# Hybrid attention and recurrence trunk: a block's value products run together, a head's first two sums run together

## The chip, the cores and the metric

One core of one Trainium2 chip runs the whole program. The metric is the device time of one execution in microseconds (us); for a kernel it is the median of its runs. A profile of one further execution gives the times of single instructions.

The engines are named as in the profile: PE is TensorE (matmuls), DVE VectorE, ACT ScalarE, POOL GpSimd, SP SyncE, which here issues DMAs alone.

## The reference, cut to what matters

Two layers over 1024 tokens of width 1024, float32. Each layer normalizes its input, projects it to 5376 columns, runs two mixers beside each other, gates and merges them, and projects back.

```python
p = jnp.exp(s - m)                                       # s: scores in windows of 128 tokens, masked
p = p / (jnp.sum(p, axis=-1, keepdims=True) + jnp.exp(sink - m))
o = jnp.einsum('bhgnqk,bnkhd->bnqhgd', p, vb)            # attention's value products, 8 heads of 64
...
decay = jnp.exp(jnp.where(causal, diff, MASK_VALUE))     # recurrence, 4 heads of 128
scores = jnp.einsum('bhtd,bhsd,bhtsd->bhts', qc, kc, decay)
o = (jnp.einsum('bhts,bhsv->bhtv', scores, vc)
     + jnp.einsum('bhtd,bhdv->bhtv', qc * jnp.exp(G), S))
...
merged = (jax.nn.sigmoid(gate_attn) * (a @ w_up_attn[layer])
          + jax.nn.sigmoid(gate_hgrn) * (b @ w_up_hgrn[layer]))
x = x + merged @ w_out[layer]
```

## The kernel before, in words

Every float32 projection is split into a high and a low part and computed as three matmuls of 128x512 into one accumulator. These are the "full" matmuls of the texts below: 128 rows and 128 columns of weights, 512 columns of data. They carry names that begin with `pi`, `pj` or `pu` in the stages of this change.

A layer goes through these stages: norm and transposes, the paired projections (`pair`), attention (`attend`, called from a loop over eight blocks of 128 tokens, together with the projection `value(u)` that makes `pi`), the four heads of the recurrence (`core`), the merge, and the output projection. In the loop over blocks, step u computes the transposes of block u-4 (`turn`), the value products of block u-4 (`values`), the scores of block u-1 and the softmax of block u-2. From block 4 on, the projections of the recurrence's first head (`pj_f`, `pj_qh`) stand beside attention in place of `pi`.

In `turn`, the probabilities of a block are transposed on PE in two groups of four heads (`tp`), group 0 and group 1, one per key-value head. ACT copies a group's transposes to `pT[:, 0]`, and DVE multiplies them with a mask into `pT[:, 1]`; in block 0 the masked one alone is used. In `values`, each group is multiplied with `vn` and `vd` (the values, and the difference of neighbouring blocks' values) into one PSUM bank `av`. An output has 64 rows, so the weights have 64 columns, and the two halves r = 0 and 1 fill the two halves of the bank.

In `core`, a head's intra-chunk scores are built level by level on DVE (`gs`, `pairs`, then `grow`), with sums over the partitions on PE. The first two of these sums (`near`, shown as `lv_n`) have a matrix of ones with 32 columns as weights: first `gs` and then `pairs` (a part of the tile `tab`), each in four quarters q. The later levels are `lv` (32 columns), `lv_m` (32), and `l` (32 and then 64). The heads are interleaved: head h starts five steps after head h-1, and the generator `filling()` gives the full matmuls of the other projections between the steps.

What sets the order: the code is written with a tile framework that keeps dependences between tiles and has a scheduler, which moves instructions of each engine ahead of one another when the operands that an instruction needs are due later. So the order on an engine isn't that of the code. At run time each engine runs its own list strictly in that order, and waits on semaphores. PSUM tiles come from two pools: `pj` (3 banks, projections) and `ps` (5 banks, all others, `av`, `sc`, `tp`, `lv_n` among them).

Of the kernel before, what the change touches and what calls it, by code (L numbers as in the profile page):

```python
# [14 lines left out]
ALU = mybir.AluOpType  # L15
AX = mybir.AxisListType

P = 128
# [6 lines left out]
HD = 64  # L25
# [15 lines left out]
def trunk_kernel(ctx, tc, x, positions, norm_w, w_in, attn_sinks, hgrn_norm_w, w_up_attn,  # L41
# [3 lines left out]
    V, S, G, PE = nc.vector, nc.scalar, nc.gpsimd, nc.tensor  # L45
# [11 lines left out]
    def slot(shape, name, dt=F32):  # L57
        return sp.tile(shape, dt, tag="slot", name=name)

    def bank(shape, name):  # L60
        return ps.tile(shape, F32, tag="bank", name=name)


    def bcast_row(row, nm):
# [6 lines left out]
    idle = slot([P, P], "idle")  # L71
    V.memset(idle, 0.0)
    zeros = bank([P, 4, P], "zeros")
    for j in range(18):
        PE.matmul(zeros[:, j % 4], lhsT=idle, rhs=idle, start=True, stop=True)
# [106 lines left out]
    def norm_turn_soon(ys, hT, hF, b0, nm, wt=None):  # L182
# [3 lines left out]
        for g in range(2):  # L186
            for b, y in enumerate(ys, b0):
                tp = bank([P, 4, P], f"tp_{nm}_{b}_{g}")
                for j in range(4):
                    k = 4 * g + j  # L190
                    PE.transpose(tp[:, j], y[:, k * P:(k + 1) * P], ident)
                tps.append((b, g, tp))
# [24 lines left out]
    def norm_turn(ys, hT, hF, b0, nm):  # L217

        n = 0
        for b, y in enumerate(ys, b0):  # L220
            a, o = b // 4, (b % 4) * P
            n += 1
            for g in range(2):
                tp = bank([P, 4, P], f"tp_{nm}_{b}_{g}")
                for j in range(4):
                    k = 4 * g + j
                    PE.transpose(tp[:, j], y[:, k * P:(k + 1) * P], ident)
                for j in range(2):
                    S.copy(hF.t[a][2 * g + j][:, :, o:o + P], tp[:, 2 * j:2 * j + 2])
        a, o = b0 // 4, (b0 % 4) * P  # L230
        t = slice(o, o + n * P)
        for kp in range(KT // 2):
            S.copy(hT.hi[a][kp][:, :, t], hF.t[a][kp][:, :, t])
            V.tensor_tensor(out=hT.lo[a][kp][:, :, t], in0=hF.t[a][kp][:, :, t],
                            in1=hT.hi[a][kp][:, :, t].bitcast(F32), op=ALU.subtract)
# [267 lines left out]
    pairs = [tuple((qkv[j][0], j) for j in js) for js in ((0, 1), (3, 2), (4, 5))]  # L503
# [11 lines left out]
    for L in range(DEPTH):  # L515
# [90 lines left out]
        other = []  # L606
# [60 lines left out]
        for g in range(2):  # L667
# [4 lines left out]
        ones, side, upper, never, mdiag, mlev, sink, hnw, lb, oml = (  # L672
            made[n] for n in "ones side upper never mdiag mlev sink hnw lb oml".split())
# [41 lines left out]
        probs = {}  # L715
# [43 lines left out]
        def turn(b):  # L759
            pr, _ = probs[b]  # L760
            probs[b] = []
            for g in range(2):

                tp = bank([P, 2, 2, P], f"tp_{L}_{b}_{g}")
                for j in range(4):
                    PE.transpose(tp[:, j % 2, j // 2], pr[:, 4 * g + j], ident)
                pT = slot([P, 2, 4, P], f"pT_{L}_{b}_{g}")
                whole = tp.rearrange("p r i q -> p (r i) q")
                if b:
                    S.copy(pT[:, 0], whole)  # L770
                V.tensor_tensor(out=pT[:, 1], in0=whole, in1=side.unsqueeze(1).broadcast_to([P, 4, P]), op=ALU.mult)
                probs[b].append(pT)

        def values(b):
            av = bank([P, 4, P], f"av_{L}_{b}")
            for g, pT in enumerate(probs.pop(b)):
                for pt in ([0, 1] if b else [1]):
                    for r in range(2):
                        PE.matmul(av[r * HD:(r + 1) * HD, 2 * g:2 * g + 2].rearrange("p h q -> p (h q)"),  # L779
                                  lhsT=(vd if b and pt else vn[0])[:, b - 1 if b else 0, g * HD:(g + 1) * HD],  # L780
                                  rhs=pT[:, pt, 2 * r:2 * r + 2].rearrange("p h q -> p (h q)"),
                                  start=pt == 0 or b == 0, stop=pt == 1)
            d = hp.tile([P, 4, P], F32, tag="po", name=f"avo_{L}_{b}")
            S.copy(d, av)
            nc.scalar.dma_start(ad[:, :, b * P:(b + 1) * P], d)

        def before(u):
            if u > 3:
                turn(u - 4)

        def attend(u):
            if u > 3:
                values(u - 4)
            if 0 < u <= NB:
                scores(u - 1)
            if 1 < u <= NB + 1:
                softmax(u - 2)
# [85 lines left out]
        def core(h):  # L883
# [3 lines left out]
            f1, R, Q = (slot([P, T], f"{n}_{nm}") for n in ("f1", "R", "Q"))  # L887
# [36 lines left out]
            def grow(hh):  # L924
# [5 lines left out]
            near = bank([P, NB, 48], f"lv_{nm}_n")  # L930
            V.tensor_tensor(out=gs, in0=R, in1=Q, op=ALU.mult)
            V.tensor_tensor(out=Q, in0=Q, in1=f1, op=ALU.mult)
            pairs = tab[:, 512:1024]
            V.tensor_tensor(out=pairs, in0=R.rearrange("p (n j) -> p n j", j=2)[:, :, 0],
                            in1=Q.rearrange("p (n j) -> p n j", j=2)[:, :, 1], op=ALU.mult)
            for src, n, o in ((gs, 32, 0), (pairs, 16, 32)):
                for q in range(4):
                    PE.matmul(near[q * 32:(q + 1) * 32, :, o:o + n], lhsT=ones,
                              rhs=src.rearrange("p (c q n) -> p q c n", q=4, n=n)[:, q], start=True, stop=True)
            yield  # L940
            V.tensor_tensor(out=acc, in0=near[:, :, 0:32], in1=mdiag.unsqueeze(1).broadcast_to([P, NB, 32]),
                            op=ALU.mult)
# [7 lines left out]
                            in0=R.rearrange("p (n i) -> p n i", i=4)[:, :, 0:2].unsqueeze(3)  # L950
                            .broadcast_to([P, T // 4, 2, 2]),
                            in1=Q.rearrange("p (n j) -> p n j", j=4)[:, :, 2:4].unsqueeze(2)
                            .broadcast_to([P, T // 4, 2, 2]), op=ALU.mult)
            lvs = bank([P, 2, NB, 32], f"lv_{nm}_1")
            for q in range(4):
                PE.matmul(lvs[q * 32:(q + 1) * 32, 0], lhsT=ones, rhs=kn[:, :, q * 32:(q + 1) * 32],
                          start=True, stop=True)
# [20 lines left out]
            for u in range(2):  # L978
                S.copy(X[u][:, :, 16:32], Qh[u][:, :, 1])
                V.tensor_tensor(out=X[u][:, :, 32:48], in0=Qh[u][:, :, 1],  # L980
                                in1=F.rearrange("p (u n j) -> p u n j", u=2, j=4)[:, u, :, 1:2]
# [3 lines left out]
            for c in range(NB):  # L985
                for q in range(4):
                    o = c * P + q * 32
                    PE.matmul(lvm[q * 32:(q + 1) * 32, c], lhsT=R[:, o:o + 32], rhs=X[c // 4][:, c % 4 * 4 + q],
                              start=True, stop=True)
# [13 lines left out]
            for c in range(NB):  # L1003
                for q in (0, 2):
                    o = c * P + q * 32
                    PE.matmul(l32[q * 32:(q + 1) * 32, c], lhsT=R[:, o:o + 32], rhs=Q[:, o + 32:o + 64],
                              start=True, stop=True)
# [5 lines left out]
            for c in range(NB):  # L1013
                o = c * P
# [15 lines left out]
            for g in range(2):  # L1030
                kv = bank([P, 4, P], f"kv_{nm}_{g}")
                n = 4 if g == 0 else 3
                for j in range(n):
                    c = 4 * g + j
                    PE.matmul(kv[:, j], lhsT=kn[:, c], rhs=it[:, c], start=True, stop=True)
                for j in range(n):
                    c = 4 * g + j
                    if c == 0:
                        V.tensor_copy(SS[:, 1], kv[:, 0])
                    else:  # L1040
                        V.scalar_tensor_tensor(out=SS[:, c + 1], in0=SS[:, c], scalar=F[:, c:c + 1],
                                               in1=kv[:, j], op0=ALU.mult, op1=ALU.add)
# [5 lines left out]
            for g in range(2):  # L1048
                po = bank([P, 4, P], f"po_{nm}_{g}")
                for j in range(4):  # L1050
                    c = 4 * g + j
# [51 lines left out]
        fill = filling()  # L1103

        heads, done = [core(h) for h in range(NHG)], 0
        for t in range(25):
            for h in range(NHG):
# [203 lines left out]
```

## Time and profile before

| | |
|---|---|
| median of 3 runs | 1406.21 us (1405.28 to 1406.41) |
| the profiled execution's own time | 1405.02 us |
| its span, first to last instruction | 1403.2 us |
| mean granted TensorE clock | 0.997 of full speed |
| busy: PE, DVE, ACT, POOL | 1379.4, 999.9, 694.6, 111.1 us |
| matmul records on PE | 8108 |
| attention, first scores to last value products, layers 1 and 2 | 328.5 to 423 us, 1017 to 1113 us |
| recurrence, first product of head 0 to last transposes of head 3 (`tb`), layers 1 and 2 | 430 to 582 us, 1120 to 1272 us |

A row of the profile's timeline has the start (us from the span's beginning), the length, the engine, the line, the operation with the tile written and the tiles read, the shape, and how many records were merged into the row; idle time of the engine before it stands in brackets. For a matmul, 128*64 is rows and columns of weights. [...] The end of a matmul is modelled and overlaps the next one's start, so the distance between starts is what a matmul takes on the queue.

### The profile page before, as it was taken

The page shows a single profiled execution, that of the slowest core. Times are in us where ns is not written, and L with a number is a line of the kernel's source. Part 1 is how long each engine was busy: PE and PEld are TensorE (multiplying, and loading weights), DVE is VectorE, ACT ScalarE, POOL GpSimd, SP SyncE. Part 2 cuts the span into 40 slices and gives each one's busy share as a digit, 9 for nine tenths or more (in the row PEclk, how much of TensorE's full clock was granted, in tenths as well). Part 3 has the DMA queues.
Part 4 walks back from the last instruction along what each step waited for, and adds up shares of the span by engine and source line. Part 5 has one row for each costly group of instructions (what it writes and reads, how often), then busy time and mean ns, then how long its engine had stood idle before and what let it go on. Part 6 is the DMA issues. An engine that isn't in the chain of part 4 may idle for free.

```text
span 1403.2 us, 21296 instructions
## 1 busy us (share of the span) xinstructions
PE 1379.4 (98%) x8108; PEld 1122.0 (80%) x8108; DVE 999.9 (71%) x1638; ACT 694.6 (49%) x1386; POOL 111.1 (8%) x195
## 2 busy tenths in 40 slices
PE   8999999999999999999999999999999999999997
PEld 7878888888777878888878888888887778788885
DVE  6867668843746879599976666776356378877998
ACT  8754334444785654313665333344358656352254
POOL 1100013220000001000010001122100000100000
PEclk9999999999999999999999999999999999999998
DMA  9434477875236651771264345587913466329203
GB/s 289 164 128 143 135 222 209 258 278 185 79 110 197 224 187 63 279 255 36 83 209 151 99 148 176 173 257 220 332 68 99 135 211 218 114 83 398 105 0 121
DMA packets 204278, 240.04 MB, mean 171 GB/s; under 512 B 14288, under 2 KB 140752, under 8 KB 204176
## 3 DMA queue, kind: packets, MB, share of 16 engines
q1 hardware_dynamic: 156528, 145.08, 31.5%
q10 hardware_dynamic: 34944, 52.44, 10.4%
q0 software_dynamic: 12704, 41.17, 9.2%
q8 instruction: 64, 1.05, 0.3%
q14 instruction: 38, 0.31, 0.1%
HBM read 160.00 MB, written 78.64 MB: 170 GB/s over the span
## 4 chain that ended last, share of the span: by engine, by line
PE 89%; ACT 4%; DVE 4%; DMA 1%; issue 1%; ACTq 0%; DVEq 0%; SPq 0%
PE pb L303 6%; PE pb L304 6%; PE pb L305 6%; PE pc L303 4%; PE pc L304 4%; PE pc L305 4%; PE pg L265 2%; PE pg L267 2%; PE pg L266 2%; PE pj_qh L141 2%; PE av L779 2%; PE pj_qh L143 2%; PE pj_qh L142 2%; PE pi L806 2%; PE pi L805 2%; PE pi L807 2%
## 5 line engine op out<-in xcount | busy, mean ns | idle before, releaser
L130 ACT CAST whi_s<-ws 128x1024 fp32r<-128x1024 f32 x30 | 31.6, 1054 | 89.4 <-PE pc L305 89.0
L314 DVE TENSOR_TENSOR pq<-pc,pq 128x512 f32<-128x512 f32 x37 | 25.5, 690 | 61.4 <-PE pc L305 56.3
L130 ACT CAST whi_o<-wo 128x1024 fp32r<-128x1024 f32 x20 | 21.1, 1055 | 78.7 <-PE pu_uh L143 35.5
L539 ACT ACTIVATE pq<-pq 128x512 f32<-128x512 f32 x60 | 37.9, 631 | 44.1 <-DVE pq L314 42.6
L141 PE MATMUL pu_ua<-wh_a,wlo_ua 128*128 128x512 f32 x128 | 52.4, 409 | 0.0
L130 ACT CAST whi_t<-ws 128x1024 fp32r<-128x1024 f32 x30 | 31.6, 1055 | 41.8 <-PE pc L305 27.9
L265 PE MATMUL pg<-hh,wl_p 128*128 128x512 f32 (+1 forms) x128 | 47.4, 373 | 4.9 <-ACT p L269 3.6
L143 PE MATMUL pu_ua<-wh_a,whi_ua 128*128 128x512 f32 x128 | 50.6, 395 | 0.0
L142 PE MATMUL pu_ua<-wl_a,whi_ua 128*128 128x512 f32 x128 | 50.4, 394 | 0.0
L131 DVE TENSOR_TENSOR wlo_s<-ws,whi_s 128x1024 fp32r<-128x1024 f32 x30 | 36.7, 1223 | 18.7 <-ACT whi_s L130 18.7
L141 PE MATMUL pu_uh<-wh_b,wlo_uh 128*128 128x512 f32 x128 | 49.8, 389 | 0.0
L143 PE MATMUL pu_uh<-wh_b,whi_uh 128*128 128x512 f32 x128 | 49.8, 389 | 0.0
L142 PE MATMUL pu_uh<-wl_b,whi_uh 128*128 128x512 f32 x128 | 49.8, 389 | 0.0
L754 ACT ACTIVATE pr<-pr,mx 128x128 f32<-128x128 f32 x128 | 49.7, 392 | 0.1
L303 PE MATMUL pb<-th,wl 128*128 128x512 f32 x120 | 47.2, 393 | 0.5 <-ACT pq L344 0.4
L303 PE MATMUL pb<-th,wlo_s 128*128 128x512 f32 x120 | 47.1, 392 | 0.0
L1001 POOL COPY scT<-acc 32x256 f32<-32x256 f32 x32 | 23.5, 734 | 296.7 <-DVE acc L995 180.6
L303 PE MATMUL pc<-hh,wlo_t 128*128 128x512 f32 x120 | 46.9, 390 | 0.0
L304 PE MATMUL pb<-tl,wh 128*128 128x512 f32 x120 | 46.8, 390 | 0.0
L305 PE MATMUL pc<-hh,whi_t 128*128 128x512 f32 x120 | 46.8, 390 | 0.0
L305 PE MATMUL pb<-th,wh 128*128 128x512 f32 x120 | 46.7, 390 | 0.0
L305 PE MATMUL pb<-th,whi_s 128*128 128x512 f32 x120 | 46.7, 390 | 0.0
(423 smaller groups left out, 4463.4 us busy)
## 6 DMA issues: line engine op xcount, KB each, us to landing
wr<-in_w_in_dram SPq DMA_DIRECT2D x72, 512.0 KB, 4.6
gd<-pq ACTq DMA_DIRECT2D x79, 256.0 KB, 3.3
fq<-fq ACTq DMA_DIRECT2D x48, 256.0 KB, 2.1
wr_p<-in_w_in_dram SPq DMA_DIRECT2D x23, 512.0 KB, 6.0
x<-in_x_dram SPq DMA_DIRECT2D x16, 512.0 KB, 6.1
qs<-qsd POOLq DMA_DIRECT2D x16, 512.0 KB, 8.2
u<-gd SPq DMA_DIRECT2D x16, 512.0 KB, 10.1
ga<-gd SPq DMA_DIRECT2D x16, 512.0 KB, 10.2
```

The costliest lines, as they stand in the source:

```text
L130: S.copy(hi, raw)
L131: eng.tensor_tensor(out=lo, in0=raw, in1=hi.bitcast(F32), op=ALU.subtract)
L141: PE.matmul(acc, lhsT=ll, rhs=rh, start=i == 0, stop=False)
L142: PE.matmul(acc, lhsT=lh, rhs=rl, start=False, stop=False)
L143: PE.matmul(acc, lhsT=lh, rhs=rh, start=False, stop=i == n - 1)
L265: PE.matmul(acc, lhsT=wl[:, k], rhs=h[:, t], start=k == 0, stop=False, skip_group_check=q > 0)
L266: PE.matmul(acc, lhsT=wh[:, k], rhs=l[:, t], start=False, stop=False, skip_group_check=q > 0)
L303: PE.matmul(acc, lhsT=wl[:, k], rhs=h, start=start and k == 0, stop=False, skip_group_check=not start)
L304: PE.matmul(acc, lhsT=wh[:, k], rhs=l, start=False, stop=False, skip_group_check=not start)
L305: PE.matmul(acc, lhsT=wh[:, k], rhs=h, start=False, stop=k == 3, skip_group_check=not start)
L539: S.activation(d, src, AF.Sigmoid if r < 2 * KT else AF.Silu)
L754: S.activation(pr[:, h], pr[:, h], AF.Exp, bias=mx[:, h:h + 1], accum_out=sm[:, h:h + 1])
```

## The change

A helper `wait_too` lets one instruction wait for a second one's result beside its own operands. It is used at two places. In `values`, blocks 0 to 5, every matmul of group 0 also waits for the masked product of group 1 (`own`), the last operand of the block. In `core`, every matmul of the first sum also waits for the product `pairs`, the operand of the second. No arithmetic and no operand changes.

```diff
+    def wait_too(ins, other):
+
+        tc.add_manual_dep(ins.ins, other.ins.name,
+                          mybir.DependencyInfo(mybir.DependencyClass.Sync, mybir.DependencyReason.DATA),
+                          reason="together")
...
-                V.tensor_tensor(out=pT[:, 1], in0=whole, in1=side.unsqueeze(1).broadcast_to([P, 4, P]), op=ALU.mult)
+                own = V.tensor_tensor(out=pT[:, 1], in0=whole, in1=side.unsqueeze(1).broadcast_to([P, 4, P]),
+                                      op=ALU.mult)
                 probs[b].append(pT)
+            probs[b].append(own)
...
-            for g, pT in enumerate(probs.pop(b)):
+            *pTs, own = probs.pop(b)
+            for g, pT in enumerate(pTs):
...
-                        PE.matmul(av[r * HD:(r + 1) * HD, 2 * g:2 * g + 2].rearrange("p h q -> p (h q)"),
+                        mm = PE.matmul(av[r * HD:(r + 1) * HD, 2 * g:2 * g + 2].rearrange("p h q -> p (h q)"),
...
+                        if g == 0 and b < 6:
+                            wait_too(mm, own)
...
-            V.tensor_tensor(out=pairs, in0=R.rearrange("p (n j) -> p n j", j=2)[:, :, 0],
+            paired = V.tensor_tensor(out=pairs, in0=R.rearrange("p (n j) -> p n j", j=2)[:, :, 0],
                             in1=Q.rearrange("p (n j) -> p n j", j=2)[:, :, 1], op=ALU.mult)
...
+                    mm = PE.matmul(near[q * 32:(q + 1) * 32, :, o:o + n], lhsT=ones,
+                                   rhs=src.rearrange("p (c q n) -> p q c n", q=4, n=n)[:, q], start=True, stop=True)
+                    if o == 0 and h > -1:
+                        wait_too(mm, paired)
```

The scheduler then makes another order. In both layers it is the same change. On PE in the attention stage, block 3 of layer 1: `av_3` are the value products of block 3 (group 0 reads `pT_3_0`, group 1 `pT_3_1`), `sc_6` the scores of block 6, `pi_7` and `pj_f` full matmuls. Before:

```order
L807 MATMUL pi_7_3476<-wh_i_6_2866,hh_1_3_179 128x512
L779 MATMUL av_3_3504<-pT_3_0_3465,vn_2689 64x256 x2
L779 MATMUL av_3_3504<-pT_3_0_3465,vd_2844 64x256 x2
L779 MATMUL av_3_3504<-pT_3_1_3473,vn_2689 64x256 x2
L730 MATMUL sc_6_0_0_3518<-ks_0_0_2870,qs_0_0_2874 128x256
L730 MATMUL sc_6_0_1_3519<-ks_0_1_2872,qs_0_1_2876 128x256
L779 MATMUL av_3_3504<-pT_3_1_3473,vd_2844 64x256 x2
L734 MATMUL sc_6_0_0_3518<-ks_0_1_2872,qs_0_0_2874 128x256
```

The same place on PE now:

```order
L149 MATMUL pj_f_0_0_0_3587<-hh_0_3_175,wh_f_0_3351 128x512
L147 MATMUL pj_f_0_1_0_3697<-hhi_0_2882,wl_f_0_3352 128x512
L788 MATMUL av_3_3504<-pT_3_0_3465,vn_2689 64x256 x2
L788 MATMUL av_3_3504<-pT_3_0_3465,vd_2844 64x256 x2
L788 MATMUL av_3_3504<-pT_3_1_3473,vn_2689 64x256 x2
L788 MATMUL av_3_3504<-pT_3_1_3473,vd_2844 64x256 x2
L736 MATMUL sc_6_0_0_3518<-ks_0_0_2870,qs_0_0_2874 128x256
L736 MATMUL sc_6_0_1_3519<-ks_0_1_2872,qs_0_1_2876 128x256
```

The four pairs of value products stand in one piece, the scores behind them, and the piece stands 25 full matmuls later.

On PE in the recurrence stage, head 3 of layer 1: `lv_3_n` are its first two sums (from `gs_3` and from `tab_3`), `l_0_2` matmuls of 64 columns of head 2, `pu_ua` full matmuls. Before, the sum from `gs_3` stood eleven full matmuls ahead of this piece:

```order
L142 MATMUL pu_ua_1_1_5011<-wl_a_1_1_4564,whi_ua_0_4805 128x512
L143 MATMUL pu_ua_1_1_5011<-wh_a_1_1_4563,whi_ua_0_4805 128x512
L1015 MATMUL l_0_2_5028<-Q_2_4630,R_2_4629 64x64
L938 MATMUL lv_3_n<-tab_3_4983,ones 32x8x16 x4
L1015 MATMUL l_0_2_5028<-Q_2_4630,R_2_4629 64x64 x7
L141 MATMUL pu_ua_2_0_5059<-wh_a_0_0_4276,wlo_ua_2_5054 128x512
```

The same place on PE now:

```order
L149 MATMUL pu_ua_1_1_5011<-wh_a_1_1_4563,whi_ua_0_4805 128x512
L147 MATMUL pu_ua_2_0_5059<-wh_a_0_0_4276,wlo_ua_2_5054 128x512
L148 MATMUL pu_ua_2_0_5059<-wl_a_0_0_4277,whi_ua_2_5053 128x512
L149 MATMUL pu_ua_2_0_5059<-wh_a_0_0_4276,whi_ua_2_5053 128x512
L949 MATMUL lv_3_n<-gs_3_4982,ones 32x8x32 x4
L949 MATMUL lv_3_n<-tab_3_4983,ones 32x8x16 x4
L1028 MATMUL l_0_2_5028<-Q_2_4630,R_2_4629 64x64 x8
```

Both sums and head 2's `l` stand in one piece, three full matmuls later than the second sum stood and fourteen later than the first.

More of the change, by code (lines that the diff above doesn't have):

```diff
@@ L937, in core @@
                 for q in range(4):
-                    PE.matmul(near[q * 32:(q + 1) * 32, :, o:o + n], lhsT=ones,
-                              rhs=src.rearrange("p (c q n) -> p q c n", q=4, n=n)[:, q], start=True, stop=True)
+                    mm = PE.matmul(near[q * 32:(q + 1) * 32, :, o:o + n], lhsT=ones,
+                                   rhs=src.rearrange("p (c q n) -> p q c n", q=4, n=n)[:, q], start=True, stop=True)
+                    if o == 0 and h > -1:
+                        wait_too(mm, paired)
             yield
```

## The prediction

> **What bounds the kernel now.** I read the page's busy times and its chain first, then the waits of TensorE, then TensorE's timeline at the two places that the change touches. Of the page:
>
> ```profile
> span 1403.2 us, 21296 instructions
> PE 1379.4 (98%) x8108; PEld 1122.0 (80%) x8108; DVE 999.9 (71%) x1638; ACT 694.6 (49%) x1386; POOL 111.1 (8%) x195
> PE 89%; ACT 4%; DVE 4%; DMA 1%; issue 1%; ACTq 0%; DVEq 0%; SPq 0%
> ```
>
> TensorE is busy for 98% of the span and makes 89% of the chain that ended last. So time taken out of TensorE's own queue comes off the end, as long as nothing it waits for becomes late. The list of its waits is short; the rows that belong to the stages of this change are
>
> ```profile
> PE tb L1068 <- DVE tab L1059: 1.3, 2, 0.7
> PE lv_n L938 <- DVE gs L931: 0.5, 1, 0.5
> ```
>
> (us in total, times, longest). In two layers of attention and recurrence TensorE stands still there for about 2 us. A busy share hides a second kind of loss, though, which is what this change is about: the price of a short run of column-tiled matmuls between full ones. TensorE's timeline around the value products (`av`, 128*64 weights) of one block shows it. Columns: start, length, line, what it does, records merged into the row. Each f32 matmul leaves two records.
>
> ```profile
> 361.14 0.39 PE L806 MATMUL pi<-wlo_i,hhi 128*128 128x512 f32 x1
> 361.46 0.65 PE L779 MATMUL av<-pT,vn 128*64 128x256 f32 x4
> 362.04 0.51 PE L730 MATMUL sc<-ks,qs 128*128 128x256 f32 x2
> 362.38 0.40 PE L734 MATMUL sc<-ks,qs 128*128 128x256 f32 x2
> 362.62 0.40 PE L730 MATMUL sc<-ks,qs 128*128 128x256 f32 x2
> ...
> 363.10 0.40 PE L807 MATMUL pi<-whi_i,hhi 128*128 128x512 f32 x1
> 363.33 0.40 PE L805 MATMUL pi<-wh_i,hl 128*128 128x512 f32 x1
> 363.66 0.65 PE L779 MATMUL av<-pT,vd 128*64 128x256 f32 x4
> 364.14 0.60 PE L779 MATMUL av<-pT,vn 128*64 128x256 f32 x4
> 364.58 0.60 PE L779 MATMUL av<-pT,vd 128*64 128x256 f32 x4
> 365.11 0.50 PE L730 MATMUL sc<-ks,qs 128*128 128x256 f32 x2
> 365.45 0.40 PE L734 MATMUL sc<-ks,qs 128*128 128x256 f32 x2
> ```
>
> Read starts, not lengths, since matmuls overlap. Undisturbed, a full matmul takes 0.23 us (363.10 to 363.33), a pair of `sc` records 0.24 (362.38 to 362.62), and four `av` records inside a run 0.44 (364.14 to 364.58). The lone run of four takes, from the full matmul ahead to the second `sc` row behind, 361.14 to 362.38 = 1.24 us. Take off 0.23 + 0.44 + 0.24 and 0.33 us is left. The run of twelve: 363.33 to 365.45 = 2.12, less 0.23 + 3 × 0.44 + 0.24, leaves 0.33. So a run of column-tiled matmuls costs a fixed third of a microsecond whatever its length. It lies on TensorE's queue in the open: about 0.09 on entry (0.32 from 361.14 to the run where 0.23 is usual), the rest inside and on the way out, where the first pair of `sc` records takes 0.34 (365.11 to 365.45) instead of 0.24.
>
> The recurrence pays the same. Head 0's two sums over the partitions (`lv_n`, 128*32 weights):
>
> ```profile
> 431.76 0.39 PE L142 MATMUL pj_f<-hl,whi 128*128 128x512 f32 x1
> 432.08 0.64 PE L938 MATMUL lv_n<-gs,ones 128*32 128x256 f32 x8
> 432.65 0.50 PE L143 MATMUL pj_f<-hh,whi 128*128 128x512 f32 x1
> 432.99 0.39 PE L141 MATMUL pj_f<-hh,wlo 128*128 128x512 f32 x1
> ...
> 434.38 0.39 PE L141 MATMUL pj_qh<-hh,wlo 128*128 128x512 f32 x1
> 434.69 0.43 PE L938 MATMUL lv_n<-tab,ones 128*32 128x128 f32 x8
> ...
> 435.39 0.39 PE L143 MATMUL pj_qh<-hh,whi 128*128 128x512 f32 x1
> ```
>
> 431.76 to 432.99 less two full matmuls is 0.77 us for the first sum, 434.38 to 435.39 less two is 0.55 for the second. By the steady rate, 0.44 and 0.22, the fixed part is again 0.33 in each.
>
> **The change part by part.** No arithmetic is added or removed; each engine issues the same instructions, and SP's and POOL's queues keep their order. What changes is the order on TensorE, and behind it on DVE and ACT.
>
> *Value products.* In program order each of blocks 0 to 5 now has one run. Runs before, by block 0 to 7: 2, 2, 4, 2, 1, 2, and 4 for blocks 6 and 7 together; that is 17 a layer. Now: six times 1, and 5 for blocks 6 and 7, which have no added wait but are cut differently; 11 a layer. Six runs × 0.33 = 2.0 us a layer.
>
> *First two sums of a head.* Heads 0 and 1: two runs become one, 0.33 each. In heads 2 and 3 the `l` matmuls (128*64 weights) of the head before join:
>
> ```profile
> 498.92 0.64 PE L938 MATMUL lv_n<-gs,ones 128*32 128x256 f32 x8
> 499.48 0.49 PE L143 MATMUL pj_qh<-hh,whi 128*128 128x512 f32 x1
> 499.91 1.15 PE L1015 MATMUL l<-Q,R 128*64 128x64 f32 x16
> 501.32 0.39 PE L142 MATMUL pj_qh<-hlo,whi 128*128 128x512 f32 x1
> 503.03 0.43 PE L938 MATMUL lv_n<-tab,ones 128*32 128x128 f32 x8
> ...
> 528.93 0.39 PE L143 MATMUL pu_ua<-wh_a,whi_ua 128*128 128x512 f32 x1
> 529.25 0.33 PE L1015 MATMUL l<-Q,R 128*64 128x64 f32 x2
> 529.65 0.43 PE L938 MATMUL lv_n<-tab,ones 128*32 128x128 f32 x8
> 531.30 0.40 PE L142 MATMUL pu_ua<-wl_a,whi_ua 128*128 128x512 f32 x1
> ```
>
> Head 2: the `l` run takes 499.48 to 501.32 less two full matmuls, 1.38, of which 0.1 is a wait (0.43 to its start where 0.32 is usual); so 1.28, and 0.95 without the fixed part. Head 3, where `l` was cut by the second sum: 528.93 to 531.30 less two is 1.91; less 0.95, 0.22 and 0.33, two changes between 64 and 32 columns cost 0.41, 0.2 each. The new run (sum, sum, `l`) has one such change: 0.44 + 0.22 + 0.95 + 0.33 + 0.2 = 2.14. It replaces 0.77 + 1.28 + 0.55 = 2.60 in head 2 and 0.77 + 1.91 = 2.68 in head 3: 0.46 and 0.54. The four heads give 0.33 + 0.33 + 0.46 + 0.54 = 1.7 us a layer.
>
> The Trainium skill (TensorEngine Tiling, section Key Properties) says that changing the tiling mode, not just the tile, drains the engine. By that rule the change from 32 to 64 columns within the new run is paid for, as the 0.2 from head 3's rows also has it; if only steps to and from the full array were paid for, the four such changes would be free and the saving 0.8 us larger. The row decides, and agrees with the rule.
>
> Both stages, both layers: 2 × (2.0 + 1.7) = 7.4 us off TensorE's queue. In all 88 runs become 66.
>
> *What the added waits cost.* A run's first matmul now needs the last operand of the whole run, and all of TensorE's queue stands behind it. What covers this is full matmuls moved ahead of the run. Rows for the last operands (DVE):
>
> ```profile
> 361.87 1.28 DVE L771 TENSOR_TENSOR pT<-tp,side 128x512 f32<-128x512 f32 x2
> 430.36 1.23 DVE L931 TENSOR_TENSOR gs<-R,Q 128x1024 f32<-128x1024 f32 x1 [6.05 <-DMA Q<-fq]
> 433.36 0.69 DVE L934 TENSOR_TENSOR tab<-R,Q 128x512 f32<-128x512 f32 x1
> 501.64 0.68 DVE L934 TENSOR_TENSOR tab<-R,Q 128x512 f32<-128x512 f32 x1
> 528.91 0.68 DVE L934 TENSOR_TENSOR tab<-R,Q 128x512 f32<-128x512 f32 x1
> ```
>
> Block 1: its run stands 11 full matmuls later than its first part did: 361.46 + 11 × 0.23 - 0.33 (block 0's saving) = 363.66; the second product ends at 361.87 + 1.28 = 363.15. Covered by 0.5. Block 0 has five full matmuls between its second transposes and its run, where it had two, and blocks 2 to 5 have 15 to 36 (3.4 us or more). Head 0: the new run stands at 434.69 - 0.77 + 14 × 0.23 = 437.1, the pair product ends at 434.05: covered. Head 2: 503.03 - 0.77 - 1.38 + 6 × 0.23 = 502.26, the product ends at 502.32: a wait of some 0.1 with its signal. Head 3: 529.25 - 0.77 + 3 × 0.23 = 529.17, the product ends at 529.59: a wait of 0.4, with the signal 0.5 (before, the second sum started 0.06 after the product's end). Head 1 lies between head 0 and head 2; I take nothing. Two layers: 2 × 0.6 = 1.2 us given back. Bounds: 0 if DVE comes earlier by as much, 3 us if every one of the 20 runs with an added wait waits 0.15.
>
> *Waits that go.* In layer 2, head 1's first sum waited for its operand:
>
> ```profile
> 1145.52 0.64 PE L938 MATMUL lv_n<-gs,ones 128*32 128x256 f32 x8 [0.53 <-DVE gs L931]
> ```
>
> It now stands 16 full matmuls (3.7 us) later, so the 0.5 goes, and so does head 2's 0.1 in each layer: 0.7, or nothing if the pair product there comes as late. Behind the runs, the next sums and transposes keep their place to within a dozen full matmuls, and from each head's `lv_m` on the order is as before but for one matmul in head 0, so the 1.3 us at `tb` stays: it depends on the distance from TensorE's own `po`, not on the clock on the wall.
>
> Sum: -7.4 + 1.2 - 0.7 = -6.9 us. The profiled execution took 1405.02 us (span 1403.2 and 1.8 around it) and would take 1398.1. The median of the three runs before is 1406.21, 1.2 above it; against that I predict 1399.3 us. The runs before spread over 1.1 us, so I take 0.2% (2.8 us) as what a measurement can tell from no change.
>
> **The rivals.**
>
> *The added waits eat half.* For: the cover at block 1 and in heads 1 to 3 is half a microsecond or less, and DVE's and ACT's orders change too. Against: nearly every run has full matmuls moved ahead of it. With 0.15 us of waiting in each of the 20 runs that got a wait, the 3 us above, and nothing gone: 1406.2 - 7.4 + 3 = 1401.8.
>
> *All cover holds, and more goes.* No new waits, the 0.7 gone and half a microsecond of small gaps with it: 1406.2 - 7.4 - 1.2 = 1397.6.
>
> *The fixed part does not go with the run.* If the 0.33 belonged to the matmuls (their first pass, say) and not to the change of tiling, joining runs would save nothing: 1406.2. Against: four and twelve records leave the same rest, and the pieces inside the twelve follow each other at 0.44.
>
> *Slower: the pair product decides.* Place: the merged sums of all eight heads. DVE's products for the two sums lie 430.36 to 434.05, 3.7 us, apart in head 0, and DVE has its other work between them. If the second is a further 2 us late in each head (three DVE operations of 0.68 put ahead of it), TensorE waits 8 × 2 = 16 us and the kernel ends at 1406.2 - 6.9 + 16 = 1415. It decides from 6.9/8 = 0.9 us a head on. Against: head 0 has 3 us to spare, and in the worst place, head 3, I find 0.5. The Trainium skill (TensorE: Matmul & The Clock Gate, Part 3) has matmuls start and end strictly in program order, so nothing behind would slip past such a wait; the row at 1145.52 agrees, since TensorE stood idle for 0.53 us there with full matmuls next in its queue.
>
> **How the numbers follow.** Forecast (1398 to 1400.6): 0.60. Half eaten (1400.6 to 1403): 0.20. More goes (below 1398): 0.10. No saving: 0.05. Slower: 0.05. The limit for faster is 1403.4, which the first and third cases keep and nine tenths of the second: 0.60 + 0.10 + 0.18 = 0.88. Within 0.2%: 0.05 + 0.02 = 0.07. Slower: 0.05. The range leaves out the last two and the far ends of the others: 1397.2 to 1402.2, its upper end the bound of 3 us plus the runs' own spread of half a microsecond.
>
> **What would show it.** Right: 66 column-tiled runs, each with a rest of about 0.33 us over the steady rates; TensorE's busy time down by some 7 us; new short waits at `lv_n` in heads 2 and 3 (under 1 us each), none at `av`. Wrong in the waits: `lv_n` or `av` high in TensorE's list of waits. Wrong in the price: the same gain missing with no waits there, the runs' rests above 0.4 us. Wrong further on: `lv`, `tn` or `tb` waiting for DVE for more than the 1.3 us of before.

## The result, and the profile after

The changed kernel took 1398.99 us (median of four runs, 1398.09 to 1400.56), the kernel before 1406.12 beside it (1405.28 to 1406.41): a ratio of 0.995, 95% interval 0.9939 to 0.9962. A second comparison gave 1397.82 against 1405.30: 0.9947 (0.9935 to 0.996). Predicted were 1399.3 us.

The page of the changed kernel, then its TensorE waits (us in total, times, longest):

```profile
span 1398.8 us, 21263 instructions
PE 1372.1 (98%) x8108; PEld 1123.6 (80%) x8108; DVE 996.6 (71%) x1638; ACT 695.6 (50%) x1386; POOL 111.0 (8%) x195
PE 85%; DVE 5%; ACT 4%; DMA 3%; issue 1%; SPq 1%; DVEq 0%; ACTq 0%
```

```profile
PE lv_n L949 <- DVE tab L945: 2.8, 5, 1.1
PE tb L1081 <- DVE tab L1072: 1.3, 2, 0.7
```

TensorE's busy time is down by 7.3 us (1379.4 to 1372.1) with the same 8108 records, and the wait at `lv_n` is up from 0.5 us to 2.8, now for `tab`, the pair product. `av` isn't in the list. (In the rows below a full matmul leaves one record, x1; the other float32 matmuls leave two.)

Block 1's value products, which were a run of four records and a run of twelve, in TensorE's timeline of the changed kernel:

```profile
363.94 0.39 PE L816 MATMUL pi<-wh_i,hl 128*128 128x512 f32 x1
364.25 0.65 PE L788 MATMUL av<-pT,vn 128*64 128x256 f32 x4
364.74 0.60 PE L788 MATMUL av<-pT,vd 128*64 128x256 f32 x4
365.17 0.60 PE L788 MATMUL av<-pT,vn 128*64 128x256 f32 x4
365.60 0.60 PE L788 MATMUL av<-pT,vd 128*64 128x256 f32 x4
366.13 0.50 PE L736 MATMUL sc<-ks,qs 128*128 128x256 f32 x2
366.47 0.40 PE L740 MATMUL sc<-ks,qs 128*128 128x256 f32 x2
```

363.94 to 366.47 is 2.53; less 0.23 for the full matmul, 4 x 0.43 for the four rows and 0.24 for the first `sc` pair, 0.34 is left, once instead of twice. This is the run's rest: what remains of its time when all its rows are taken off at their steady rates.

Heads 2 and 3 of the recurrence, TensorE:

```profile
501.24 0.39 PE L148 MATMUL pj_qh<-hl,whi 128*128 128x512 f32 x1
501.62 0.64 PE L949 MATMUL lv_n<-gs,ones 128*32 128x256 f32 x8
502.08 0.40 PE L949 MATMUL lv_n<-tab,ones 128*32 128x128 f32 x8
502.41 1.15 PE L1028 MATMUL l<-Q,R 128*64 128x64 f32 x16
503.48 0.50 PE L149 MATMUL pj_qh<-hh,whi 128*128 128x512 f32 x1
503.82 0.40 PE L147 MATMUL pj_qh<-hh,wlo 128*128 128x512 f32 x1
...
527.61 0.39 PE L149 MATMUL pu_ua<-wh_a,whi_ua 128*128 128x512 f32 x1
528.44 0.64 PE L949 MATMUL lv_n<-gs,ones 128*32 128x256 f32 x8 [0.44 <-DVE tab L945]
528.89 0.40 PE L949 MATMUL lv_n<-tab,ones 128*32 128x128 f32 x8
529.23 1.15 PE L1028 MATMUL l<-Q,R 128*64 128x64 f32 x16
530.30 0.50 PE L147 MATMUL pu_ua<-wh_a,wlo_ua 128*128 128x512 f32 x1
530.64 0.39 PE L148 MATMUL pu_ua<-wl_a,whi_ua 128*128 128x512 f32 x1
```

The merged run of head 2 is 503.82 - 501.24 less two full matmuls, 2.12 us, of which 0.06 is a wait. In head 3 it is 2.57, 0.5 of it the wait (the step to the run is 0.83 where 0.32 is usual).

Head 1 of layer 1, where no wait was expected. TensorE, then DVE:

```profile
457.40 0.39 PE L147 MATMUL pj_f<-hh,wlo 128*128 128x512 f32 x1
458.93 0.64 PE L949 MATMUL lv_n<-gs,ones 128*32 128x256 f32 x8 [1.14 <-DVE tab L945]
```

```profile
454.62 1.23 DVE L942 TENSOR_TENSOR gs<-R,Q 128x1024 f32<-128x1024 f32 x1 [1.30 <-DMA Q<-fq]
...
458.10 0.68 DVE L945 TENSOR_TENSOR tab<-R,Q 128x512 f32<-128x512 f32 x1
```

TensorE stood for 1.2 us; DVE itself had stood for 1.3, for the load of Q. The pair product ends 4.2 us after `gs` starts; in head 1 it does so in the profile before and in both layers here.

### The profile page after: what moved, and what is told of

It is laid out like the page before. It is cut to its first block, busy times and chain, and to the rows that moved or that the text cites. A ratio compares the mean times of both kernels' runs of the same rounds, so it can differ in the third digit from the quotient of the medians.

```text
span 1398.8 us, 21263 instructions
## 1 busy us (share of the span) xinstructions
PE 1372.1 (98%) x8108; PEld 1123.6 (80%) x8108; DVE 996.6 (71%) x1638; ACT 695.6 (50%) x1386; POOL 111.0 (8%) x195
## 4 chain that ended last, share of the span: by engine, by line
PE 85%; DVE 5%; ACT 4%; DMA 3%; issue 1%; SPq 1%; DVEq 0%; ACTq 0%
PE pb L309 6%; PE pb L311 6%; PE pb L310 6%; PE pc L309 4%; PE pc L311 4%; PE pc L310 4%; PE pg L271 2%; PE pg L273 2%; PE pg L272 2%; PE pi L817 2%; PE pi L816 2%; PE av L788 2%; PE pi L818 2%; PE pu_uh L149 2%; PE pu_uh L148 2%; PE pu_uh L147 2%
## 5 line engine op out<-in xcount | busy, mean ns | idle before, releaser
L310 PE MATMUL pc<-hl,whi_t 128*128 128x512 f32 x120 | 46.7, 389 | 0.0
```

Source lines behind the costliest of these rows:

```text
L310: PE.matmul(acc, lhsT=wh[:, k], rhs=l, start=False, stop=False, skip_group_check=not start)
```

## The experiments

Theory: a column-tiled run between full matmuls costs 0.33 us once, and what the merging gives back is TensorE's wait for the pair product. Rivals: the price belongs to the matmuls and not to the run; the gain comes from one part or from the new order at large; the waits cost more than they show.

**Each part alone (av_alone, sums_alone).** The one leaves the sums as before, the other the value products:

```diff
-                    if o == 0 and h > -1:
+                    if o == 0 and h > 9:
```

```diff
-                        if g == 0 and b < 6:
+                        if g == 0 and b < 0:
```

> The value products of blocks 0 to 5 run together, the first two sums of a head stay as before; 76 column-tiled runs against 88 before and 66 in the changed kernel. Theory (each run between full matmuls costs 0.33 us once): 12 runs fewer x 0.33 = 4.0 us off, 1402.1 us, with lv_n's waits as before (0.5 us in all) and no wait at av. Rival (the price belongs to the matmuls): no saving, 1406.1. Rival (the gain is that of the whole new order, not of the runs): anything else, such as under 2 us off.

> The first two sums of a head run together, the value products stay as before; 78 column-tiled runs. Theory: 3.4 us off for the runs, less the waits that TensorE gets at lv_n. If those waits come from this part alone they are 2.8 us as in the changed kernel (0.5 before): 3.4 - 2.3 = 1.1 off, 1405.0 us. If head 0's and head 1's waits come because the later value products push the projections of the first head back, they are about 1.2 us here: 2.7 off, 1403.4. Rival (the price belongs to the matmuls): slower by the waits, 1407 to 1408.

Measured: 1402.35 and 1403.66 us, before 1405.72 beside them: 3.4 us off (ratio 0.9977, 0.9968 to 0.9986) and 2.1 off (0.9984, 0.9975 to 0.9992). Both parts gain. Their TensorE waits at `lv_n`, of av_alone first:

```profile
PE lv_n L949 <- DVE gs L942: 1.2, 1, 1.2
```

```profile
PE lv_n L949 <- DVE tab L945: 1.5, 4, 0.4
```

In av_alone, too, head 1 stood still for 1.2 us, for `gs` itself, with nothing merged there: a late load of Q is paid for with or without the merged sums. In sums_alone, which came out near the second of its two cases (1403.4), head 0 doesn't wait in either layer, and head 1 for 0.4 and 0.3 us: head 0's wait in the changed kernel comes with the value products. The two gains add up to 5.4 us against 7.1 and 7.5 of the whole; by the intervals the parts are worth 2.0 to 4.5 and 1.1 to 3.5, the whole in its second comparison 5.6 to 9.1, so that they do more together than apart isn't shown.

**The price of a run (cut_full, cut_64; one_128, one_64).** An extra matmul, whose result is overwritten, stands within each run of value products, once with 128 columns of weights, which cuts the run, once with 64, which doesn't:

```diff
+                    if g == 0 and b < 6:
+                        cut = PE.matmul(av[0:128, 2], lhsT=ident[:, 0:128], rhs=pT[:, 1, 0], start=True, stop=True)
+                        behind(cut, mm)
```

(`behind` sets the order on the engine and no wait; the kernels with 64 have `av[0:64, 2]` and `ident[:, 0:64]`.) In the first pair the loop over the halves r was put outside that over `pt`, so that two cuts could stand in each block.

> The changed kernel with each run of value products of blocks 0 to 5 cut twice by one full float32 matmul of 128x128 whose result is overwritten (24 in all; a block's halves are computed one after the other, r outside). 88 column-tiled runs. To be read against the next one, which differs only in that its 24 extra matmuls have 64 columns of weights. Theory: 24 x 0.33 = 7.9 us slower than that one; 24 x (0.22 + 0.33) = 13 us slower than the changed kernel, 1412. Rival (the price belongs to the matmuls): within 1 us of that one, 1404 to 1405.

> As the one before, but the 24 extra matmuls have 64 columns of weights, so that the runs are not cut: 64 column-tiled runs. Theory and rival: the matmuls themselves, 24 x 0.06 to 0.22 us = 1.4 to 5.3 us over the changed kernel, 1400.4 to 1404.3; the new order of the halves is taken as free.

Measured: 1421.93 and 1405.23 us, 16.7 apart where 7.9 was expected. Both are slower than was foretold (1412, and 1400.4 to 1404.3). In cut_64 a block's run takes 2.37 us up to `sc`, where the changed kernel's takes 1.88 (364.25 to 366.13): 0.24 for each of the extra matmuls, about 5.7 for the 24. The timeline of cut_full, TensorE, one block:

```profile
378.50 0.39 PE L153 MATMUL pj_f<-hl,wh_f 128*128 128x512 f32 x1
378.81 0.65 PE L794 MATMUL av<-pT,vn 128*64 128x256 f32 x2
379.30 0.59 PE L794 MATMUL av<-pT,vd 128*64 128x256 f32 x2
379.82 0.49 PE L804 MATMUL av<-pT,ident 128*128 128x128 f32 x2
...
381.67 0.66 PE L794 MATMUL av<-pT,vn 128*64 128x256 f32 x4
382.15 0.61 PE L794 MATMUL av<-pT,vd 128*64 128x256 f32 x4
382.69 0.50 PE L741 MATMUL sc<-ks,qs 128*128 128x256 f32 x2
383.03 0.40 PE L745 MATMUL sc<-ks,qs 128*128 128x256 f32 x2
```

Here a row of two records, all of one half, takes as long as a row of four with both halves: 378.81 to 379.82 is 1.01 for four records, 381.67 to 382.69 is 1.02 for eight. The two halves of a block, which write different partitions, run side by side when they follow each other, and the cut between them undid that. The block takes 4.53 us; less 0.23 and 0.24 at its ends, three pieces of 0.86 and two cuts of 0.22, 1.04 is left for three runs, 0.35 each. So the price of a run stands, but the pair couldn't show it by its times. The second pair has one cut a block, between the groups, with the halves side by side.

> The changed kernel with one full float32 matmul of 128x128 (its result is overwritten) between the two groups of value products of blocks 0 to 5, 12 in all; the halves stay side by side, which they did not in the first such kernel. 78 column-tiled runs. Against the next kernel, whose extra matmuls have 64 columns: theory 12 x (0.33 + 0.22 - 0.25) = 3.6 us slower (0.22 the two records of such a matmul on the full array, 0.25 those of one with 64 columns within a run), 6.6 over the changed kernel. Each of the two pieces of a block then has a rest of 0.33 us. Rival (the price was that of the lost side-by-side work of the halves, not of the cut): within 1 us of the next kernel.

> As the one before, with 64 columns of weights in the 12 extra matmuls: the runs stay whole, 66 of them. 12 x 0.25 = 3 us over the changed kernel, about 4 to 4.5 under before.

Measured: 1407.03 and 1402.67 us, 4.4 apart. TensorE in one_128, then in one_64:

```profile
378.97 0.39 PE L154 MATMUL pj_f<-hh,wh_f 128*128 128x512 f32 x1
379.29 0.65 PE L794 MATMUL av<-pT,vn 128*64 128x256 f32 x4
379.77 0.60 PE L794 MATMUL av<-pT,vd 128*64 128x256 f32 x4
380.30 0.49 PE L803 MATMUL av<-pT,ident 128*128 128x128 f32 x2
380.72 0.65 PE L794 MATMUL av<-pT,vn 128*64 128x256 f32 x4
...
382.07 0.40 PE L745 MATMUL sc<-ks,qs 128*128 128x256 f32 x2
```

```profile
376.50 0.39 PE L154 MATMUL pj_f<-hh,wh_f 128*128 128x512 f32 x1
...
379.25 0.40 PE L745 MATMUL sc<-ks,qs 128*128 128x256 f32 x2
```

3.10 us less 0.23, 1.73, 0.22 and 0.24 leaves 0.68, twice 0.34. The uncut block takes 2.75, of which its one run's rest is 0.34 and the extra matmul 0.21 (its run takes 2.09 up to `sc`, the changed kernel's 1.88). So a cut costs 0.35 a block, 12 x 0.35 = 4.2 us, beside 4.4 measured and 3.6 expected. one_64 itself came 3.2 us under before, not 4 to 4.5; its profile has a wait of 2.6 us at `lv_n`, where before has 0.5. The rival that the price belongs to the matmuls falls: in cut_full, too, each run has the same rest, whether it holds two records (in block 0), four or eight, and an added run brings another 0.34.

**The waits (after_again, late1, late13).** The changed kernel again, and two kernels in which a head's sums are queued behind the `l` matmuls of the head before: in head 1, or in heads 1 and 3.

```diff
+                        if h == 1:
+                            tc.add_manual_dep(mm.ins, LAST[0], mybir.DependencyInfo(
+                                mybir.DependencyClass.NoSync, mybir.DependencyReason.DATA), reason="late")
```

(`LAST[0]` is the last 64-column `l` matmul; the sums are written one step later. late13 has `h % 2`.)

> The changed kernel once more, beside before in as many rounds, since its four runs spread over 2.5 us and each part alone gave 3.4 and 2.1 us, 5.5 together. If the parts add up: 5.5 us under before. If the median of the first four runs stands: 7.1 under. In its profile the wait of head 1's first sum in layer 1 (1.3 us) is either there again (its cause is the order) or differs by over 0.5 us (its cause is the time that the load of Q takes in that execution).

> The changed kernel, with head 1's two sums queued behind head 0's last l matmuls (they stand behind those and two full matmuls more, in one run with l). Theory (head 1's run waits for the pair product because it stands too early on TensorE): the waits of head 1 (1.3 us in layer 1, 0.6 in layer 2) go, and two runs become one in each layer with one 32/64 change, 2 x (0.33 - 0.2) = 0.3 us: about 2 us under the changed kernel in the profiled spans, 1 to 2 in the medians. Rival (the pair product's lateness sets what follows anyway): the wait turns up at head 1's next sum lv, 0.5 us or less is gained.

> Head 1's and head 3's sums queued behind the l matmuls of the head before. Theory: head 3's waits (0.5 us in each layer, the same in both profiles of the changed kernel since its load of Q has long landed) go as well; span about 1 us under late1's 1395.7, and TensorE waits at lv_n for under 0.5 us in all. Rival (DVE is late for what follows too): a wait at head 3's next sum lv of 0.3 us or more in each layer. The medians can hardly tell 1 us; the profile decides.

Measured: 1397.82, 1398.29 and 1398.56 us, ratios 0.9947, 0.9947 and 0.9945: not to be told apart. The 1 to 2 us that late1 was to gain in the medians didn't come; its span was 1.8 us under that of after_again (1395.7 and 1397.5). The profiles say why. after_again, TensorE's waits, its head 1 in layer 1 and DVE there:

```profile
PE lv_n L949 <- DVE tab L945: 1.0, 3, 0.4
```

```profile
457.18 0.39 PE L147 MATMUL pj_f<-hh,wlo 128*128 128x512 f32 x1
457.54 0.64 PE L949 MATMUL lv_n<-gs,ones 128*32 128x256 f32 x8
```

```profile
453.23 1.23 DVE L942 TENSOR_TENSOR gs<-R,Q 128x1024 f32<-128x1024 f32 x1
...
456.71 0.69 DVE L945 TENSOR_TENSOR tab<-R,Q 128x512 f32<-128x512 f32 x1
```

The same program, and the wait of 1.2 us is gone: the load of Q was issued 0.75 us sooner (448.21 against 448.96) and took 4.9 us instead of 5.6, so that DVE hardly waited for it (0.1 us). So most of head 1's wait is the lateness of a transfer in one execution, and late1 had little left to take: in its profile too the load was early, the sums stood 1.85 us behind the pair product, with no wait in head 1 (0.1 us at the `lv` behind them). In late13's profile the load was late again. DVE and TensorE, head 1 in layer 1, and two rows of TensorE's waits:

```profile
457.59 0.68 DVE L946 TENSOR_TENSOR tab<-R,Q 128x512 f32<-128x512 f32 x1
...
459.63 1.23 DVE L969 TENSOR_TENSOR f<-R,Q 128x1024 f32<-128x1024 f32 x1
```

```profile
458.87 0.64 PE L952 MATMUL lv_n<-gs,ones 128*32 128x256 f32 x8
...
460.96 0.64 PE L976 MATMUL lv<-f,ones 128*32 128x256 f32 x8 [0.81 <-issue]
```

```profile
PE lv L976 <- issue: 1.2, 2, 0.8
PE l L1035 <- DVE R L929: 0.9, 4, 0.2
```

The sums didn't wait, and the next sum `lv` stood for 0.8 us instead. The profile names no releaser there, but its operand `f`, DVE's product three operations behind the pair product, ends at 460.86, 0.1 us before it starts: what is late is passed on, as the rival had it. Head 3's wait of 0.5, which was there in both profiles of the changed kernel, did go in late13, without a wait at its `lv`. But not all of it was gained: the `l` matmuls of head 2, which now come first in that run, waited for DVE's `R` in both layers, for which they hadn't in the changed kernel (4 waits at `l`, there 2). That lost 0.3 us of each 0.5. late13's span was 1398.7, not 1 us under late1's 1395.7.

**More merging (av_all, all_late1, seven_late13).** `b < 8` in place of `b < 6`, alone and with late1's change; and `b < 7` with late13's.

> The value products of blocks 6 and 7 run together as well; 58 column-tiled runs against 66. Theory: 8 x 0.33 = 2.6 us under the changed kernel, no wait at av (block 7's run has 18 full matmuls ahead of it since the one before). Rival (the last blocks have no cover, and the projection behind them feeds head 0 later): a wait at av of 0.5 us or more in each layer or a wait of head 0's sums, so that the gain is under 1 us.

> Both additions, the value products of all eight blocks together and head 1's sums behind head 0's l. Theory: the two gains add, about 4 us under the changed kernel (1395). Rivals as for the two parts: between 1396 and 1399.

> As late13, with block 6's value products together too (blocks 0 to 6), block 7's not. Theory of the loss in av_all (its block 6 and 7 runs put off head 0's load of Q from 425.6 to 428.5 us): if block 7 did it, head 0 waits for 0.2 us or less and 0.7 us more than late13 is gained; if the later run of block 6 is enough, head 0's sums wait for 1 us or more in each layer and the kernel ends 1 to 2 us over late13.

Measured: 1400.41 (0.9964, 0.995 to 0.9978), 1399.46 (0.9964, 0.9952 to 0.9977) and 1397.73 us (0.9942, 0.9929 to 0.9954). av_all saves eight runs more (six of value products; two because head 1's sums fell in with `l` by themselves), was to gain 2.6 us, and is 2.6 us behind the changed kernel run beside it, as its rival had it. all_late1, put at 1395, missed in the same way: head 0's sums waited for 1.4 and 0.7 us, and head 1's `lv` for about 0.5 in each layer. Head 0 of av_all in layer 1, DVE and TensorE:

```profile
432.24 1.23 DVE L942 TENSOR_TENSOR gs<-R,Q 128x1024 f32<-128x1024 f32 x1 [8.54 <-DMA Q<-fq]
```

```profile
436.07 0.64 PE L949 MATMUL lv_n<-gs,ones 128*32 128x256 f32 x8 [1.62 <-DVE tab L945]
```

The load of Q was issued at 428.47 (425.63 in after_again), and the sums stand 35 full matmuls behind the value products where they had 47, so TensorE came sooner to an operand that came later. In layer 2 head 0 waited for 0.9. From the store that it waits for (issued at 423.50, and 422.89) to the load it took 5.0 us instead of 2.7; what held that store up isn't settled. In seven_late13 head 0's waits were 0.4 and 0.7, between the two cases expected. It has the lowest median and the lowest span (1395.2), but its interval covers the changed kernel's ratio: no version is shown to beat it.

**The account.** All these profiles can be put to one sum. The two stages, from the first `sc` to the last `tb` of each layer, took 253.21 and 253.80 us before. In the table, "runs" is 0.34 us for each run fewer and 0.1 for each 32/64 change more (there were four before, and there are four or six now; the 0.1 is worked out in the next section). "Waits" is what TensorE lost at the first matmul of a run of `lv_n`, `lv` or `l` beyond the usual step of 0.32, against 1.4 before; all in us against before.

| kernel | runs | waits | sum | stages measured | median |
|---|---|---|---|---|---|
| changed | -7.5 | +2.6 | -4.9 | -5.2 | -7.1 |
| changed, again | -7.5 | +0.9 | -6.6 | -6.9 | -7.5 |
| av_alone | -4.1 | +0.7 | -3.4 | -3.7 | -3.4 |
| sums_alone | -3.4 | +1.3 | -2.1 | -2.5 | -2.1 |
| late1 | -8.0 | +0.7 | -7.3 | -7.8 | -7.0 |
| late13 | -8.0 | +1.6 | -6.4 | -6.8 | -7.3 |
| av_all | -10.0 | +4.5 | -5.5 | -4.8 | -4.9 |
| all_late1 | -10.0 | +3.6 | -6.4 | -5.8 | -5.8 |
| seven_late13 | -8.6 | +1.5 | -7.1 | -7.6 | -8.1 |

Runs and waits give each stage time to within 0.7 us. The medians follow the stages to within 0.8 us, but for the changed kernel's first comparison, whose profile was the slowest of its runs.

## Why the prediction was right, point by point

*The runs.* 88 became 66, and each one's rest is 0.34 us by the rows above, where 0.33 was taken. TensorE's busy time fell by 7.3 us where 7.4 was summed.

*The 32/64 change: a term too large.* The merged run was put at 2.14 us. Less its wait it took 2.06 in head 2 (2.12 less 0.06) and 2.07 in head 3 (2.57 less 0.5). Without any price for the change it would be 1.94, so the change from 32 to 64 columns within the run costs 0.1 and not 0.2. The 0.41 for two changes was read from a run in which the second sum also waited for its product, 0.06 by the prediction's own account; less that, they took 0.17 each. As there are four changes before and four after, the total hardly moves. The Trainium skill (TensorEngine Tiling, section Key Properties) has every change of the tiling mode drain the engine; head 2's row agrees, since without a price the run would take 1.94, and it took 2.06.

*Value products.* 2.0 us a layer. From the first `sc` to the first `lv_m` the profile fell from 118.45 to 116.51 us in layer 1 (328.52 to 446.97, and 329.12 to 445.63), 1.94. Head 0's saved run (0.33) is in it, and against it its wait (0.28) and one full matmul more (0.23), which leaves 2.1. No run waited, as said.

*Waits in heads 2 and 3.* Put at 0.1 and 0.5 us; 0.06 and 0.5 in both profiles and both layers. Here both sides moved alike: counted from the first `sc`, head 2's run came 1.3 us sooner than the working had it, and so did its pair product.

*Waits in heads 0 and 1: the step that failed.* "Covered" for head 0 and "I take nothing" for head 1. Measured were 0.3 and 0 in head 0 and 1.2 and 0.6 in head 1 (layers 1 and 2) in the first profile, and 0.2, 0, 0.05 and 0.2 in the second. The working moved TensorE's run later by the full matmuls put ahead of it, but the time that merged runs further ahead save it took off at block 1 alone. Ahead of head 0 these are the six runs of value products, 2.0 us. In the first profile head 0's run would have begun at 435.6 without its wait. Counted from the first `sc`, which comes 0.6 us later there, that is 2.2 us sooner than the 437.1 of the working. The pair product hangs on the load of Q, which didn't come sooner: by the same count it was issued 0.25 us later and took 6.2 us instead of 5.4, and the product ended 1.1 us later (435.72). So the 3 us to spare were used up. In layer 2 TensorE came as much sooner, but the load took 5.1 us, and 1.0 us of cover was left. For head 1 the same count gives a wait from rows of before: its first sum's start, 455.67, plus 16 full matmuls (3.7) less the saved 2.0 and 0.33 is 457.0, and the pair product ended at 458.16, 1.2 us later. In layer 2 this count gives 2.0 us; there the load came sooner too, and 0.6 was measured. The upper bound for all waits, 3 us, was just passed in the first profile (3.2) and not in the second (1.6). By its own sign the prediction was wrong in the waits: `lv_n` stands second in the first profile's list.

*Waits that go.* 0.7 was taken off, "or nothing if the pair product there comes as late". It did in part: head 1's wait in layer 2 was 0.6 again in the first profile, 0.2 in the second. Head 2's 0.1 at `l` went.

*Profile and median.* In the profiled execution the time fell by 4.4 us (spans 1403.2 and 1398.8), in the medians by 7.1, as its profile is the slowest of the four runs (1400.56) and holds head 1's 1.2 us. The stages alone fell by 5.2; the other 0.8 lies where the kernels don't differ. In the second profile the stages fell by 6.9, the sum that was predicted, and the span by 5.7. That the median met the forecast to 0.3 us is in part luck: the waits of two profiles of one program differ by 1.6 us, and about 1 us lies outside the stages.

The rival "waits eat half" was the nearest to the first profile (1401.8 foretold, 1400.56 measured for that execution), not to the median. The slower one, the pair product, stayed at 0.2 to 0.4 us a head on the mean, against the 0.9 from which it would decide. In av_all it came to 0.65 us a head (5.2 us in all), which ate more than the extra runs saved.

## What to carry to other kernels

Count the runs of column-tiled matmuls between full ones and price each at the rest that the timeline shows (0.34 us here), since a busy share of 98% hides it. Before joining two runs, ask when the last operand comes and what it hangs on in turn. Count the cover from the consumer's new time, earlier by all that the change saves ahead of it, and not to the operand's old time, but through its producer to the transfer behind it, which a merge further up can move. A wait that one profile shows and a second of the same program doesn't is no property of the order, so take two before you spend an edit on it.

## What the runs showed of the hardware that was not expected

Matmuls on the two halves of the columns run side by side: in cut_full a run of four records of one half takes 1.01 us up to the next matmul (378.81 to 379.82), and a run of eight records, four of each half, 1.02 (381.67 to 382.69). The Trainium skill (TensorE: Matmul & The Clock Gate, Part 3) says that small matmuls on different tiles of the array run concurrently, which these rows agree with. So a full matmul put between the halves costs the lost overlap beside the run's price: 16.7 us for 24 cuts, where 12 cuts between groups cost 4.4.

The load of Q took from 3.7 to 7.4 us from issue to landing within the first profiled execution of the changed kernel, and head 1's in layer 1 differed by 0.65 us between two executions of the same program (5.6 us from 448.96, and 4.9 from 448.21). There is little room for that: in the first profile seven of the eight merged sums start 0.05 to 0.15 us behind the end of their pair product, and only head 0's in layer 2 had cover left, 1.0 us.
